# Four modulation quarters: from the end of the front to the head of the stream order

## The chip, the cores and the metric

The kernel runs on one core of a Trainium2 chip, as one launch, with float32 inputs and outputs. The metric is the device time of that launch in microseconds (us). Three runs of the kernel before gave 1077.91, 1078.41 and 1078.48 us; their median is 1078.41 us. One further execution was profiled, and all profile rows of "before" come from it.

The engines are called as in the profile: PE multiplies matrices (PEld loads its weights), DVE works on whole tiles elementwise, ACT applies functions and copies, POOL does a few small operations and issues some transfers, SP issues most transfers. Each engine works through its own list in order; a semaphore wait at the head of a list holds everything behind it.

## The reference, cut to what matters

One layer of a diffusion backbone for 512 latent tokens and 256 context tokens, width 1024:

```python
m_lat = (jax.nn.silu(c) @ mod_w[layer] + mod_b[layer])[:, None, :]     # 1024 x 6144
sh1, sc1, g1, sh2, sc2, g2 = jnp.split(m_lat, 6, axis=-1)
h_lat = rms_norm(x, norm_mix_g) * (1.0 + sc1) + sh1
mix   = token_mixer(h_lat, h_ctx, ...)    # gated DeltaNet (A) and HGRN2 (B), both directions, 4 heads each
x = x + g1 * mix
x = x + g2 * swiglu(rms_norm(x, norm_ffn_g) * (1.0 + sc2) + sh2, ffn_w_in, ffn_w_out)
return rms_norm(x, final_norm_g)
```

The modulation row `m_lat` is the product of one vector with the 1024 x 6144 matrix `mod_w`. Its first two sections (sh1, sc1) are needed at the start, to make `h_lat`. The other four are needed late: g1 (section 2) after the mixer, sh2 and sc2 (3, 4) before the feed-forward part, g2 (5) at the end. These are the **late modulation**. Each section is cut into four **quarters** of 256 columns; a quarter reads 1 MB of weights.

## The kernel before, in words

**Products.** Every large product is done as three passes over a high and a low part of both operands (`mm3`). A weight tile is loaded by SP into `raw`, cast by ACT into `hi` (L103), and DVE makes `lo = raw - hi` (L105); rings of two buffers each.

**The front** (L179 to L407) loads x, ctx and the early part of `mod_w`, makes sh1 and sc1 on PE (`pmod`), makes the normed and modulated tokens transposed (`hhi`, `hlo` for the latent tokens, `chi`, `clo` for the context), and multiplies as it goes six column blocks of the merge gates (`pg0`). At its end, with a priority lowered by 1500, two more gates (22 and 23, tiles `rw`) are multiplied, and then come the four quarters of section 2 (g1). Then the small decay parameters are made (L411 to L468: `pab`, `la`, `dec`).

**A quarter** (`mod_now`) is one transfer of 1 MB, ten DVE operations of 128 x 256 (two products L165, six multiply-adds L167, one sum L168, and the addition to the bias `vc` L176), and in between a short group of PE instructions that sum over partitions (`pmo`, L119) into the PSUM bank "fa". There is one bank "fa"; the low-priority gates (`gate_low`) accumulate in it too. In the front a quarter's transfer is issued by SP, and its tile is one of the six buffers "mw" of the front's pool `s1`. A quarter called by `mod_early` is issued by POOL, and its tile is the single buffer "aT" or "N" of the pool `gd`. These two are otherwise the attention and decay matrices of the DeltaNet pair in work.

**The streams.** After the front, generators are advanced by the string `PLAN`, written out by hand: G0 and G2 are the DeltaNet heads 0, 1 and 2, 3; H0 to H3 the HGRN2 heads; F is a low-priority gate; N and aT are single quarters in those tiles. One number is how many steps are taken. What stands earlier in PLAN has the higher priority. The first six steps of a G stream are the projections k, q, v of two heads with a five-tap convolution and SiLU (DVE L665, L670, L679; ACT L656 to L691); a POOL `memset` clears the borders of each `pad` tile first. Then N and aT are built (L724 to L735), inverted by a recursion on DVE (L754, L756), and six steps over the chunks follow.

**What sets the order.** A list planner simulates the program at build time and fixes the order of each engine's list: among what is ready in its simulation, the highest priority goes first. In its order, a pool that takes the room of an earlier one opens after that one has been finished altogether; the waits left in the program are finer, tile by tile. So the tiles of `fl`, `hg` and `gd` (the streams) are first written, in the planner's order, after the last instruction on the front's pools `s1`, `sp` and `s3`. Within a pool, the buffers lie in the order in which the program first asks for their names. In the kernel before, `gd` begins with KT, QT, Vt, and N and aT come after the convolution buffers ("cv", "blk"). At the end of the streams, `gd` gives its room to `wx` (weights of the remaining gates, loaded by SP), `md` (the remaining quarters, loaded by POOL in halves `mwb`, L906) and `x1p`.

**After the streams:** the gates' remainder, up-projections, output projection, and the feed-forward part, which are bounded by PE.

Of the kernel before, what the change touches and what calls it, by code (L numbers as in the profile page):

```python
# [7 lines left out]
F32 = mybir.dt.float32  # L8
# [5 lines left out]
P = 128  # L14
D = 1024
KT = 8
# [13 lines left out]
PADQ = 8 * 68  # L30
MK = 4

PLAN = ("H0:1 G0:6 F:1 H1:3 G0:4 F:1 G2:3 G0:5 F:2 N:1 G0:1 H0:2 "
        "F:1 G0:99 H0:99 F:3 G2:4 H1:99 G2:4 F:1 G2:99 N:1 H3:99 aT:1 H2:1 X H2:99")


# [15 lines left out]
def body(tc, T, out, tap=None):  # L52
    nc = tc.nc
# [7 lines left out]
    with ExitStack() as root:  # L61
        def pool(name, bufs=1, side=None, **kw):
            return tc.tile_pool(name=name, bufs=bufs, side=side, reuse_waits="tile", **kw)
# [57 lines left out]
        def feat(w, src, n, name, t0=0, tag="mm"):  # L121

            ps = bank(tag, name)
            mm3(ps[:, 0:n], [lambda k, t=t: t[:, k, :] for t in w], [lambda k, t=t: t[:, k, t0:t0 + n] for t in src], KT)
            return ps
# [11 lines left out]
        def gate_out(i, ps, pool, tag="raw"):  # L137
            gt = pool.tile([P, SEQ], F32, name=f"gt{i}", tag=tag, bufs=3 if pool is ring.get("sp") else 2)
            nc.scalar.copy(gt[:, :], ps[:, :])
            nc.sync.dma_start(gdram[i, :, :], gt[:, :])  # L140
# [15 lines left out]
        quarters = [(sec, j) for sec in (2, 3, 4) for j in range(4)]  # L156

        def mod_now(sec, j, mw, queue):

            c0 = D * sec + 256 * j  # L160
            queue.dma_start(mw[:, 0:KT, :], T["mod_w"][0, :, c0:c0 + 256].rearrange("(k p) f -> p k f", p=P))
            for k in range(KT):
                acc = mw[:, k % 2, :]
                if k < 2:
                    nc.vector.tensor_scalar_mul(acc, acc, sc[:, k:k + 1])  # L165
                else:
                    nc.vector.scalar_tensor_tensor(acc, mw[:, k, :], sc[:, k:k + 1], acc, op0=ALU.mult, op1=ALU.add)  # L167
            nc.vector.tensor_tensor(mw[:, 0, :], mw[:, 0, :], mw[:, 1, :], op=ALU.add)  # L168
            mod_sum(sec, j, mw[:, 0, :], "fa")

        def mod_sum(sec, j, acc, tag):
            ps = bank(tag, f"pmo{sec}{j}")
            for i in range(2):
                column_sums(ps, i, acc[:, P * i:P * i + P])
            c = 8 * sec + 2 * j
            nc.vector.tensor_tensor(mbc[:, c:c + 2], ps[:, 0:2], mbc[:, c:c + 2], op=ALU.add)  # L176
# [7 lines left out]
        with ExitStack() as st:  # L184
            s1 = st.enter_context(pool("s1"))
# [216 lines left out]
            for i in rest[0:2]:  # L402
                w = [s1.tile([P, KT, P], F32R, name=f"rw{i}{j}") for j in range(2)]
                w = split([W_IN[:, gcols[i]:gcols[i] + P]], KT, P, dst=[t[:, :, :] for t in w])
                gate_out(i, feat(w, lat, SEQ, f"pgate{i}"), sp, "gt")
            for q in quarters[0:4]:
                mod_now(*q, s1.tile([P, KT, 256], F32, name="mwe%d%d" % q, tag="mw", bufs=6), nc.sync)  # L407
            del quarters[0:4]
            tc.cur_priority -= 1500


# [551 lines left out]

        before, after = PLAN.split("X")
        for item in before.split():
            name, n = item.split(":")
# [26 lines left out]
        for item in after.split():  # L993
            name, n = item.split(":")
# [222 lines left out]
```

## Time and profile before

| | before |
|---|---|
| median of three runs | 1078.41 us (1077.91 to 1078.48) |
| the profiled execution | 1083.86 us |
| its span, first to last instruction | 1082.1 us |
| PE busy / DVE busy / ACT busy | 1013.3 / 648.6 / 551.6 us |
| mean clock granted to PE | 0.978 |

In a row of busy time by stretch, the numbers are the stretch and its length, then for each engine the busy time and, in brackets, the count of instructions; then the clock granted to PE, the share of the transfer engines, and GB/s. In a row of the timeline, they are the start, the length, the engine, the line in the kernel, the operation, what it writes and reads, and, in square brackets, how long the engine had been idle and what ended that. "SPq" is SP issuing a transfer. A row "x6" merges six instructions in a row.

### The profile page before, as it was taken

To read this page: it belongs to the slowest core of one execution; us is meant where nothing else is said; L and a number is where in the kernel's file an instruction comes from. 1 tells how busy PE (TensorE), PEld (TensorE's weight loads), DVE (VectorE), ACT (ScalarE), POOL (GpSimd) and SP (SyncE) were. 2 spreads that over 40 slices of the span, in tenths; PEclk is the share of its full clock that TensorE was granted. 3 is DMA by queue.
4 is the path that set the end of the run, shared out by engine and by line. 5 is a ranking of instruction groups with operands and counts; after the bars stand their busy time and mean duration, and the time that the engine had idled before them with its cause. 6 is when DMAs were issued, how large, how long until landed. Compare 5 with 4: busy or idle time off the path is not lost.

```text
span 1082.1 us, 18148 instructions
## 1 busy us (share of the span) xinstructions
PE 1013.3 (94%) x7255; PEld 830.2 (77%) x7255; DVE 648.6 (60%) x1258; ACT 551.6 (51%) x1053; POOL 72.7 (7%) x129
## 2 busy tenths in 40 slices
PE   4999999889998899899979999999999999999996
PEld 2577888777797687788758788797888878888785
DVE  3375686789666858965786575686343434322524
ACT  3372678558976775786764643442222222221212
POOL 1000000400011012001111000010000000000000
PEclk9999999989999899999998999999999999999998
DMA  9953212113013122201647743445333323333222
GB/s 316 334 182 114 57 48 78 42 48 89 12 51 108 50 69 69 69 3 58 214 129 232 257 153 125 129 151 180 97 98 97 97 80 98 98 98 97 89 97 88
DMA packets 139656, 121.73 MB, mean 112 GB/s; under 512 B 5661, under 2 KB 116531, under 8 KB 139571
## 3 DMA queue, kind: packets, MB, share of 16 engines
q1 hardware_dynamic: 133923, 103.96, 31.4%
q0 software_dynamic: 3552, 13.11, 3.7%
q10 hardware_dynamic: 2096, 3.50, 1.0%
q8 instruction: 57, 0.93, 0.3%
q14 instruction: 28, 0.23, 0.1%
HBM read 110.07 MB, written 10.49 MB: 111 GB/s over the span
## 4 chain that ended last, share of the span: by engine, by line
PE 65%; DVE 12%; ACT 8%; issue 6%; DMA 5%; POOL 2%; SPq 0%; POOLq 0%; DVEq 0%; ACTq 0%
PE pf L113 20%; PE pfo L113 10%; PE h_z L113 5%; PE pgate L113 4%; PE pg L369 3%; PE pup L113 3%; DVE lo L105 2%; PE g_q_zl L113 2%; DMA mwb<-in_mod_w_dram 2%; PE pwo L113 1%; PE g_k_zl L113 1%; DVE p_o L754 1%; PE p_pD L724 1%; ACT hi L103 1%; DVE p_Z L756 1%
## 5 line engine op out<-in xcount | busy, mean ns | idle before, releaser
L103 ACT CAST hi<-raw 128x1024 fp32r<-128x1024 f32 (+1 forms) x129 | 127.6, 991 | 277.3 <-PE pf L113 98.1
L105 DVE TENSOR_TENSOR lo<-raw,hi 128x1024 fp32r<-128x1024 f32 (+1 forms) x129 | 147.8, 1147 | 174.2 <-ACT hi L103 173.9
L113 PE MATMUL pf<-hhi,lo 128*128 128x512 f32 (+1 forms) x352 | 133.8, 380 | 0.5 <-DVE lo L105 0.5
L113 PE MATMUL pf<-hhi,hi 128*128 128x512 f32 (+1 forms) x352 | 133.8, 381 | 0.0
L113 PE MATMUL pf<-hlo,hi 128*128 128x512 f32 (+1 forms) x352 | 133.7, 380 | 0.0
L113 PEld LDWEIGHTS pf<-hhi,lo 128*128 128x128 f32 x352 | 66.2, 188 | 13.7 <-DVE lo L105 1.1
L113 PEld LDWEIGHTS pf<-hlo,hi 128*128 128x128 f32 x352 | 66.2, 188 | 12.5 <-DVE hlo L1097 0.2
L113 PEld LDWEIGHTS pf<-hhi,hi 128*128 128x128 f32 x352 | 66.1, 188 | 12.4
L113 PE MATMUL pfo<-lo,uh 128*128 128x512 f32 x176 | 68.8, 391 | 0.1
L113 PE MATMUL pfo<-hi,ul 128*128 128x512 f32 x176 | 68.5, 389 | 0.0
L113 PE MATMUL pfo<-hi,uh 128*128 128x512 f32 x176 | 67.9, 390 | 0.0
L113 PE MATMUL pgate<-hhi,lo 128*128 128x512 f32 x128 | 54.3, 425 | 6.4 <-DVE lo L105 6.4
L113 PE MATMUL pgate<-hhi,hi 128*128 128x512 f32 x128 | 54.1, 423 | 4.0 <-ACT hi L103 3.9
L113 PE MATMUL pgate<-hlo,hi 128*128 128x512 f32 x128 | 53.0, 414 | 0.0
L1153 DVE TENSOR_TENSOR sg<-sg,pf 128x512 f32<-128x512 f32 x22 | 15.1, 687 | 49.4 <-PE pf L113 49.3
L908 DVE SCALAR_TENSOR_TENSOR acc<-mwb,sc,acc 128x256 f32<-128x256 f32 x72 | 34.2, 480 | 12.6 <-DMA mwb<-in_mod_w_dram 11.5
L113 PE MATMUL h_z<-hhi,hi 128*128 128x512 f32 x96 | 38.6, 402 | 1.3 <-ACT h_Z L515 1.3
L113 PEld LDWEIGHTS pfo<-lo,uh 128*128 128x128 f32 x176 | 33.0, 188 | 7.8 <-DVE lo L105 1.0
L113 PEld LDWEIGHTS pfo<-hi,uh 128*128 128x128 f32 x176 | 32.8, 188 | 7.4 <-ACT hi L103 0.7
L113 PEld LDWEIGHTS pfo<-hi,ul 128*128 128x128 f32 x176 | 33.0, 188 | 6.8
L113 PE MATMUL h_z<-hlo,hi 128*128 128x512 f32 x96 | 37.9, 395 | 0.0
L113 PE MATMUL h_z<-hhi,lo 128*128 128x512 f32 x96 | 37.7, 392 | 0.0
(453 smaller groups left out, 2471.9 us busy)
## 6 DMA issues: line engine op xcount, KB each, us to landing
raw<-in_ffn_w_in_dram SPq DMA_DIRECT2D x44, 512.0 KB, 3.7
raw<-in_w_in_dram SPq DMA_DIRECT2D x37, 512.0 KB, 3.7
raw<-in_ffn_w_out_dram SPq DMA_DIRECT2D x22, 512.0 KB, 3.6
mwb<-in_mod_w_dram POOLq DMA_DIRECT2D x18, 512.0 KB, 4.8
mw<-in_mod_w_dram SPq DMA_DIRECT2D x16, 512.0 KB, 6.0
gdram<-gt SPq DMA_DIRECT2D x24, 256.0 KB, 2.1
raw<-in_w_in_dram SPq DMA_DIRECT2D x18, 256.0 KB, 3.0
mwe<-in_mod_w_dram SPq DMA_DIRECT2D x4, 1024.0 KB, 7.9
```

The costliest lines, as they stand in the source:

```text
L103: nc.scalar.copy(hi[:, :, :], raw[:, :, :])
L105: nc.vector.tensor_tensor(lo[:, :, :], raw[:, :, :], hi.bitcast(F32), op=ALU.subtract)
L113: nc.tensor.matmul(ps, a[u](k), b[v](k), start=(start and n == 0), stop=(stop and n == tot - 1))
L369: nc.tensor.matmul(pg0[i][:, :], u[:, P * i:P * i + P], v[:, d, :], start=(d == 0 and n == 0), stop=(d == KT - 1 and n == 2))
L724: nc.tensor.matmul(pD[:, P * d:P * d + P], (LS, US)[d], lu[:, d, :], start=True, stop=True)
L754: nc.vector.tensor_tensor(ov, Z[:, r + 1:32, r:r + 1].to_broadcast([P, 31 - r, r]), Z[:, r:r + 1, 0:r].to_broadcast([P, 31 - r, r]), op=AL ...
L756: nc.vector.tensor_tensor(Z[:, r + 1:32, 0:r], Z[:, r + 1:32, 0:r], ov, op=ALU.add)
L908: nc.vector.scalar_tensor_tensor(acc[:, :], mw[:, k - k0, :], sc[:, k:k + 1], acc[:, :], op0=ALU.mult, op1=ALU.add)
L1153: nc.vector.tensor_tensor(sg[:, :], sg[:, :], pgu[1][:, :], op=ALU.mult)
```

## The change

The four quarters of section 2 are taken out of the front, and four items are put into PLAN behind H0's first step: one quarter in the tile aT, one in N, and two more in aT. The last four lines of the front that issue them go; the two gates above them stay.

```diff
-PLAN = ("H0:1 G0:6 F:1 H1:3 G0:4 F:1 G2:3 G0:5 F:2 N:1 G0:1 H0:2 "
+PLAN = ("H0:1 aT:1 N:1 aT:2 G0:6 F:1 H1:3 G0:4 F:1 G2:3 G0:5 F:2 N:1 G0:1 H0:2 "
         "F:1 G0:99 H0:99 F:3 G2:4 H1:99 G2:4 F:1 G2:99 N:1 H3:99 aT:1 H2:1 X H2:99")
...
                 gate_out(i, feat(w, lat, SEQ, f"pgate{i}"), sp, "gt")
-            for q in quarters[0:4]:
-                mod_now(*q, s1.tile([P, KT, 256], F32, name="mwe%d%d" % q, tag="mw", bufs=6), nc.sync)
-            del quarters[0:4]
             tc.cur_priority -= 1500
```

The items call a function that was there already:

```python
def mod_early(sec, j, tag):
    mod_now(sec, j, gd.tile([P, 12 if tag == "N" else KT, 256], F32, name=f"mwe{sec}{j}", tag=tag), nc.gpsimd)
```

The list `quarters` is used up in the same order as before, so that the later items N:1, N:1, aT:1 and the remaining quarters are the same ones in both kernels. What moves with a quarter is its transfer (from SP's list to POOL's), its DVE operations, its PE sums, and its tile (from `s1` to `gd`). "aT" and "N" become the first names asked for in `gd`, so every buffer of `gd` up to "blk" gets another place.

## The prediction

> **What bounds the kernel now.** The page first, for the span, the busy shares, the chain that ended last and one kind of transfer.
>
> ```profile
> span 1082.1 us, 18148 instructions
> ...
> PE 1013.3 (94%) x7255; PEld 830.2 (77%) x7255; DVE 648.6 (60%) x1258; ACT 551.6 (51%) x1053; POOL 72.7 (7%) x129
> ...
> PE 65%; DVE 12%; ACT 8%; issue 6%; DMA 5%; POOL 2%; SPq 0%; POOLq 0%; DVEq 0%; ACTq 0%
> ...
> raw<-in_w_in_dram SPq DMA_DIRECT2D x37, 512.0 KB, 3.7
> ```
>
> PE is busy 94% and holds 65% of the chain: time is lost only where PE stands idle or does more. So I went on to busy time by stretch around the change, and one row for what follows.
>
> ```profile
> 70.00:80.00 10.00, 10.00 (x52) 7.72 (x51) 9.92 (x28) 10.00 (x20) 0.00 (x0) 1.00 1.01 327
> ...
> 100.00:110.00 10.00, 9.26 (x75) 8.02 (x75) 3.69 (x7) 5.48 (x10) 0.00 (x0) 0.86 0.30 88
> 110.00:120.00 10.00, 10.00 (x57) 8.77 (x56) 5.63 (x6) 5.99 (x9) 0.00 (x0) 1.00 0.18 52
> 120.00:140.00 20.00, 19.00 (x182) 16.12 (x181) 13.84 (x22) 13.36 (x20) 1.77 (x9) 1.00 0.19 54
> 140.00:160.00 20.00, 20.00 (x149) 16.71 (x148) 16.99 (x26) 16.12 (x25) 1.80 (x4) 1.00 0.19 53
> ```
>
> ```profile
> 200.00:300.00 100.00, 90.66 (x1063) 73.72 (x1063) 82.25 (x177) 73.33 (x149) 12.62 (x24) 0.95 0.17 46
> ```
>
> PE has no idle time from 70 to 80 us, 0.74 us in 100 to 110, 1.0 us in 120 to 140; DVE has much room before 120 and little after (13.84 and 16.99 of 20 us). In 200 to 300 DVE is at 82% and PE loses 9.3 us, in the recursion on DVE: what G0 loses before that is not simply given back there. Next, the same stretches for the quarters' tiles alone, then the timeline where front and streams meet.
>
> ```profile
> 60.00:70.00 10.00, 0.00 (x0) 0.00 (x0) 2.12 (x7) 0.00 (x0) 1.00 0.21 56
> 70.00:80.00 10.00, 0.00 (x0) 0.00 (x0) 4.75 (x13) 0.00 (x0) 1.00 1.01 327
> 80.00:90.00 10.00, 0.00 (x0) 0.00 (x0) 3.62 (x9) 0.00 (x0) 1.00 0.69 222
> 90.00:100.00 10.00, 0.60 (x30) 0.43 (x30) 3.87 (x9) 0.00 (x0) 0.97 0.16 45
> ```
>
> ```profile
> 96.73 0.31 PE L119 MATMUL pmo<-ones,mwe 128*32 128x1 f32 x16
> ...
> 97.18 0.20 DVE L458 TENSOR_TENSOR la<-e,nal 128x48 f32<-128x48 f32 x1
> ...
> 97.45 0.34 SPq L140 DMA_DIRECT2D gdram<-gt  x1
> ...
> 97.55 0.62 PE L465 MATMUL pg<-la,sq 128*128 128x24 f32 x4
> ...
> 103.43 1.05 ACT L103 CAST hi<-raw 128x1024 fp32r<-128x1024 f32 x1 [4.03 <-PE h_z L113]
> ...
> 103.44 0.22 PE L119 MATMUL pmo<-ones,mwe 128*32 128x1 f32 x2
> 103.70 0.16 DVE L176 TENSOR_TENSOR vc<-pmo,vc 128x2 f32<-128x2 f32 x1 [6.32 <-PE pmo L119]
> ...
> 104.38 0.85 ACT L515 COPY h_Z<-h_z 128x512 f32<-128x512 f32 x2
> ...
> 104.50 0.31 PE L119 MATMUL pmo<-ones,mwe 128*32 128x1 f32 x16 [0.29 <-DVE vc L176]
> ...
> 105.01 0.50 PE L113 MATMUL g_k_zl<-hhi,hi 128*128 128x512 f32 x1 [0.20 <-ACT h_Z L515]
> ```
>
> The quarters take 2.12 + 4.75 + 3.62 + 3.87 = 14.36 us of DVE, **3.59 us each**, nearly all while PE has other work. They cost PE two gaps in its own work: 96.73 to 97.55, and 103.44 to 105.01, where their sums stand between the last context product and G0's first projection, each waiting until DVE has emptied the bank of the one before.
>
> **The change part by part.**
>
> **1. Front, PE.** The two stretches go: 0.82 + 1.57 = 2.39 us. The sums themselves stay PE work: four groups of about 0.31 us (the group at 104.50) = 1.24 us, now put between G0's projections, where they wait only if bunched. Net -1.15. For the second stretch there is a condition: 105.01 also waits for ACT's copy of `h_Z` (104.38), which clears the PSUM bank. That copy is the first write into the stream pools, so in the planner's order it comes after everything on the front's pools; the last of that now is the fourth quarter's sum, afterwards it is gate 23's store, issued at 97.45. Then the copy no longer stands behind the cast at 103.43, which had to wait for PE. If it doesn't move, the second stretch is kept and the term is 0.82 - 1.24 = +0.4; if it moves, and H0's and G0's starts with it, as far as the copy can (104.38 back to the store, 97.45: 6.9 us) and half of that reaches the end, -3.5. I take -1.15, because PE is full before and after and can only gain what it did there.
>
> **2. The first two quarters.** Their tiles aT and N become the lowest in `gd`, and by the order of names they lie where the buffers of the early `mod_w` (`mw`) lay.
>
> ```profile
> L313 PE MATMUL pmod<-mw,sch x80: 592/617/1061, 13.7 to 52.8; 128*32 128x512 f32 x48, 128*32 128x256 f32 x32
> ```
>
> PE read those for the last time at 52.8 us, so POOL can issue both loads as soon as its list is past the power at 62.39:
>
> ```profile
> 62.39 0.65 POOL L299 TENSOR_TENSOR ss<-ss,mhalf 128x1 f32<-128x1 f32 x1 [6.32 <-DVE ss L298]
> ...
> 509.04 0.96 POOL L161 DMA_DIRECT2D mwe<-in_mod_w_dram  x1 [0.68 <-PE p_s_pk L864]
> 510.74 1.02 POOL L478 TENSOR_TENSOR p_hs<-p_hs,mhalf 128x4 f32<-128x4 f32 x1 [0.73 <-DVE p_hs L477]
> ...
> 518.02 2.40 POOL L478 TENSOR_TENSOR p_hs<-p_hs,mhalf 128x4 f32<-128x4 f32 x1 [5.36 <-DVE p_hs L477]
> ```
>
> A load from POOL took 509.04 to 515.26 = 6.22 us (next fence). Both are in at about 70. The planner puts their DVE work just behind `la` (97.18), which comes up to 3.87 us sooner, since the stretch 90 to 100 loses that much DVE work. DVE then has 97.38 - 3.87 = 93.5 to 103.70 free (the row at 103.70 shows 6.32 idle): 10.2 us for 7.18. Cost **0**, hidden by the h_z products on PE. If the cover is gone (loads only after the front, landing at 97.45 + 6.2), the 7.18 us fall in 104 to 111 and cost up to that less the DVE idle of 100 to 110 (6.31): +0.9.
>
> **3. The last two quarters.** Both need the one buffer aT, so each waits for the sum of the one before: load (6.22), DVE (3.59), sum, load. From a first sum at about 107, the third's DVE work starts near 114, the fourth's near 125: in the middle of G0's convolutions. There it has priority over all G0 work, being earlier in PLAN, and DVE's list is in order. What a quarter loaded late does to DVE's list the trace shows at the end of the streams:
>
> ```profile
> 515.26 0.62 DVE L165 TENSOR_SCALAR mwe<-mwe,sc 128x256 f32<-128x256 f32 x2 [3.99 <-DMA mwe<-in_mod_w_dram]
> ...
> 520.99 0.62 DVE L165 TENSOR_SCALAR mwe<-mwe,sc 128x256 f32<-128x256 f32 x2 [1.46 <-DMA mwe<-in_mod_w_dram]
> ...
> 528.58 0.15 DVE L176 TENSOR_TENSOR vc<-pmo,vc 128x2 f32<-128x2 f32 x1
> ```
>
> DVE stood 3.99 us for one and 1.46 us for the other before the data was there: the planner expected them sooner. Bounds for the wait 0 and 3.99; I take the mean, 2.7, the two rows being equally near. A late quarter thus holds DVE 3.59 + 2.7 = 6.3 us, both **12.6 us**. Queued behind on DVE are the five-tap convolutions and the `lo` parts, for which ACT and PE wait, as G0's norm sum shows:
>
> ```profile
> 127.25 0.39 PE L113 MATMUL pgate<-hhi,hi 128*128 128x512 f32 x1
> ...
> 134.25 0.43 PE L119 MATMUL g_q_pn<-ones,g_q_acc 128*32 128x1 f32 x32 [0.88 <-ACT g_q_acc L691]
> ```
>
> ```profile
> 100.00:200.00 100.00, 1.83 (x6) 0.98 (x6) 0.00 (x0) 0.99 0.22 62
> ```
>
> Cover: DVE's idle time in 110 to 140 is 4.37 + 6.16 = 10.5 us, but in pieces between operations that depend on each other; I count half, 5.3. Lower bound of the term: all of it used and no landing wait, 7.18 - 10.5 < 0, so 0. Upper: none used and 3.99 each, 15.2. Mine: 12.6 - 5.3 = 7.3. PE has no slack against this chain: at 134.25 it already stands 0.88 us for it. What PE can do meanwhile is the low gate, begun at 127.25. In 100 to 200 it got six products (the last row, gates alone); of its first half, 12 products, six are left, by 13.68 us for 52 (term 4's rows) 0.26 us each, 1.6 us. So **+5.7**.
>
> POOL's list: behind the two late loads stand `memset`s of the `pad` tiles and the powers for G0's norms; each load waits there for the sum before it, and the planner puts it at about that time. No cost of its own; 0 to the length of one delay, inside the bounds above.
>
> On loads from POOL, what the sum does not need. The Trainium skill ("DMA: Bandwidth & Descriptors", Anatomy of one DMA — SWDGE (gpsimd) path) fits 2.0 us + bytes / 436e3 per us, an estimate of 4.4 us for 1 MB; the trace has 6.22, so I keep that, and by the page the term would be about 2 x 1.8 us less. It also states ("SBUF — State Buffer", Who interferes with whom) that a DVE operation in a two-port mode, which `tensor_scalar` can enter, shuts POOL out of its port, descriptors included: the power at 518.02 took 2.40 us during a quarter's DVE work against 1.02 at 510.74, which agrees, and by it the two late loads could be issued 1.4 us later each while DVE is at work.
>
> **4. End of the streams.** The buffers of `wx` now lie over aT and N, and not over KT, QT, Vt. The remaining gates' first load must wait until quarter (3, 2) in aT is summed (528.58, above) and not only for its turn in SP's list:
>
> ```profile
> 523.24 1.88 SPq L95 DMA_DIRECT2D raw<-in_w_in_dram  x2
> ```
>
> That is 5.3 us later. The gates are first multiplied after 540:
>
> ```profile
> 520.00:540.00 20.00, 0.00 (x0) 0.00 (x0) 0.00 (x0) 0.91 0.65 196
> 540.00:560.00 20.00, 13.68 (x52) 9.22 (x52) 1.15 (x2) 1.00 0.50 157
> ```
>
> A load of that kind lands 3.7 us after issue (last row of the first fence), 532.3, with the cast (1.05 at 103.43) and a `lo` of about as much 534.4: **0**, hidden by PE's other work in 520 to 540. Without that cover +5.3. `md`, for its part, no longer lies over N, and may load some us earlier: I know no row for that and leave it at 0, with as much as the load's 5.3 in the other direction as its bound.
>
> **Sum:** -1.15 + 0 + 5.7 + 0 = +4.55 us, against the profiled execution: 1083.86 to 1088.4. The profiled execution is 5.45 us over the median of the runs, 1078.41; the difference carries over: **1083.0 us**.
>
> **The rivals.**
>
> *Hidden after all, 1077.8.* The two late quarters fall into DVE's idle pieces and the planner lets H1's products (next in PLAN) run ahead on PE. For it: 10.5 us of idle against 7.18. Against: the rings of two buffers and the `pad` tiles, which DVE must free, bound how far PE runs ahead. Then only -1.15 and about +0.5 of bunched sums remain.
>
> *Faster, 1074.4.* One mechanism: the front's pools end with gate 23's store and not with the fourth sum, so that H0's copies, G0's first `pad` tiles and G0's first projection start earlier. Place 97 to 105, price -2.39 to -3.5 (term 1), plus up to -0.5 from DVE in 70 to 80, where it is 9.92 of 10 us busy and the context's `lo` parts wait among the quarters. It decides if the late quarters cost the G0 chain under 2 us. For it: PE is full before and after, so PE's gain stays a gain. Against: term 3.
>
> *Twice as slow, 1088.7.* The low gate takes the bank "fa" at 127.25, before the fourth quarter's sum. Then that sum waits for the gate's 18 remaining products (4.7 us), its copy and the sum (1 us), and G0's own aT waits with it:
>
> ```profile
> 187.70 0.41 DVE L735 TENSOR_TENSOR p_aT<-p_E,p_pD 128x256 f32<-128x256 f32 x1
> ```
>
> Before, all four sums were out by 105, ahead of the gate. Here +4.55 + 5.7.
>
> **How the numbers follow.** Forecast 0.45 (1080.6, where no change ends, to 1085.6, with landing waits of 3.99), hidden 0.20, faster 0.20, bank 0.15. What a measurement of this kernel can tell from no change is about 0.2%, 2.2 us. Faster: 0.20 and a little of hidden, 0.23. Same: the rest of hidden and the low end of the forecast, 0.22. Slower: 0.55. Range: from the faster rival's 1074.4 to the bank's 1088.7 and the 2.6 us of longer landing waits, 1074.4 to 1091.
>
> **What would show it.** Right: the first two quarters' DVE work between 93 and 105, loads issued by POOL at about 63; G0's first projection at 102 to 104 instead of 105.01; two runs of quarter work on DVE between 110 and 135 with idle in front ended by their transfer; the sum that stood at 134.25 later by 3 us or more, with more PE idle in 120 to 200. Wrong: those two runs in DVE time that was idle, PE idle in 100 to 200 no larger (hidden, or faster); the loads of the first two only after 97; a sum `pmo` after 180 (bank); or a difference that arises after 500, by term 4.

## The result and the profile after

| | before | after |
|---|---|---|
| median | 1078.45 us (4 runs, 1077.91 to 1079.05) | 1088.05 us (4 runs, 1086.56 to 1090.56) |
| ratio, 95% interval | 1 | 1.0091 (1.0068 to 1.0115) |
| the same again, beside later experiments | 1080.37 us | 1.0102 (1.0081 to 1.0123) |
| the profiled execution, its span | 1083.86, 1082.1 us | 1090.56, 1088.8 us |

The change makes the kernel slower by 9.6 us. The forecast was 1083.0, 4.55 us slower: the sign and the range held, the size was half of it. The profiled executions differ by 6.7 us only; that of before lies 5.4 us over its median, that of after 2.5.

First the busy time of the kernel after by stretch, in the columns of before.

```profile
70.00:80.00 10.00, 7.18 (x32) 5.24 (x31) 3.99 (x10) 6.97 (x14) 0.00 (x0) 0.90 0.98 301
...
100.00:110.00 10.00, 10.00 (x60) 8.87 (x60) 1.98 (x3) 6.21 (x11) 0.16 (x2) 1.00 0.15 47
110.00:120.00 10.00, 10.00 (x86) 8.22 (x84) 9.96 (x23) 5.40 (x8) 1.11 (x5) 1.00 0.34 106
120.00:140.00 20.00, 13.02 (x140) 10.54 (x133) 16.42 (x34) 8.51 (x13) 1.98 (x6) 0.83 0.40 122
140.00:160.00 20.00, 20.00 (x134) 16.76 (x133) 16.46 (x26) 13.42 (x21) 0.87 (x7) 1.00 0.25 67
```

Set against the rows of before, PE has lost 2.82 us in 70 to 80 and 5.98 us in 120 to 140 (13.02 for 19.00), and there the granted clock is 0.83 for 1.00. It has gained 0.74 us in 100 to 110, where the granted clock is 1.00 for 0.86. From 140 to 160 PE is as full as before; from 160 to 200 it loses another 0.8 us. What ended PE's idle time, in us, times, and the longest, for the two places:

```profile
PE pc L264 <- ACT gt L139: 2.8, 1, 2.8
```

```profile
PE pmo L119 <- DVE mwe L168: 4.2, 1, 4.2
PE g_v_zl L113 <- DVE lo L105: 2.2, 1, 2.2
PE g_v_zc L113 <- ACT g_q_pad L653: 0.5, 1, 0.5
```

Now the timeline after, at the first of the two places:

```profile
62.88 2.12 POOL L161 DMA_DIRECT2D mwe<-in_mod_w_dram  x2
...
66.65 1.50 SPq L95 DMA_DIRECT2D raw<-in_w_in_dram  x2
...
70.37 8.13 SPq L140 DMA_DIRECT2D gdram<-gt  x6
...
73.96 1.05 ACT L103 CAST hi<-raw 128x1024 fp32r<-128x1024 f32 x1 [1.26 <-DMA raw<-in_w_in_dram]
...
76.33 1.82 ACT L139 COPY gt<-pg 128x512 f32<-128x512 f32 x3 [1.33 <-DMA gdram<-gt]
```

POOL issues both loads at 62.88, as forecast. But then ACT waits for a gate weight loaded by SP (1.26 us) and for a store that has to leave its buffer (1.33 us), and PE waits for ACT. In the second place:

```profile
110.93 0.96 DVE L519 SCALAR_TENSOR_TENSOR h_sg<-h_Z,h_sg 128x768 f32<-128x768 f32 x1
...
111.81 0.61 DVE L165 TENSOR_SCALAR mwe<-mwe,sc 128x256 f32<-128x256 f32 x2
...
116.08 0.88 POOL L161 DMA_DIRECT2D mwe<-in_mod_w_dram  x1 [13.01 <-PE pmo L119]
...
121.84 0.62 DVE L165 TENSOR_SCALAR mwe<-mwe,sc 128x256 f32<-128x256 f32 x2 [0.33 <-DMA mwe<-in_mod_w_dram]
...
125.71 0.42 DVE L168 TENSOR_TENSOR mwe<-mwe 128x256 f32<-128x256 f32 x1
...
126.18 0.40 PE L119 MATMUL pmo<-ones,mwe 128*32 128x1 f32 x16 [4.23 <-DVE mwe L168]
...
127.55 1.22 DVE L105 TENSOR_TENSOR lo<-raw,hi 128x1024 fp32r<-128x1024 f32 x1
...
128.83 0.79 PE L113 MATMUL g_v_zl<-hhi,lo 128*128 128x512 f32 x1 [2.25 <-DVE lo L105]
...
132.58 0.62 DVE L165 TENSOR_SCALAR mwe<-mwe,sc 128x256 f32<-128x256 f32 x2 [0.47 <-DMA mwe<-in_mod_w_dram]
...
137.45 0.30 PE L119 MATMUL pmo<-ones,mwe 128*32 128x1 f32 x16
...
144.32 0.43 PE L119 MATMUL g_q_pn<-ones,g_q_acc 128*32 128x1 f32 x32
```

The first two quarters' DVE work runs at 111.81, 49 us after its data was asked for and behind H0's `h_sg`, not at 93 to 105. The third quarter arrives almost on time (0.33 us of waiting), but PE comes to its sum in its list 4.23 us before DVE has it. Behind it stands `lo` at 127.55, a weight of G0's next product, for which PE waits another 2.25 us. G0's norm sum, which stood at 134.25, is at 144.32: **10.07 us late**, and most of that stays to the end.

### The profile page after: what moved, and what is told of

Read it like the earlier page. It is cut to its first block, busy times and chain, and to the rows that moved or that the text cites. A ratio compares the mean times of both kernels' runs of the same rounds, so it can differ in the third digit from the quotient of the medians.

```text
span 1088.8 us, 18157 instructions
## 1 busy us (share of the span) xinstructions
PE 1007.9 (93%) x7255; PEld 824.2 (76%) x7255; DVE 650.3 (60%) x1258; ACT 552.3 (51%) x1053; POOL 77.5 (7%) x133
## 4 chain that ended last, share of the span: by engine, by line
PE 60%; DVE 13%; DMA 8%; ACT 8%; issue 7%; POOL 2%; SPq 1%; POOLq 0%; DVEq 0%; ACTq 0%
PE pf L113 18%; PE pfo L113 10%; PE pg L369 3%; PE pup L113 3%; PE h_z L113 3%; PE pgate L113 3%; DMA mwb<-in_mod_w_dram 3%; DVE lo L105 2%; PE g_v_zl L113 2%; PE g_k_zl L113 2%; PE g_q_zl L113 1%; DVE p_o L751 1%; PE p_pD L721 1%; DMA mwe<-in_mod_w_dram 1%; DVE p_Z L753 1%
```

## The experiments

Three points in each trace (one profiled execution of each kernel) tell where time goes: G0's first projection on PE, its norm sum on PE (`g_q_pn`), and the stretch between them, which is the time that the streams' first steps take. The last column is the timed ratio to before, with its interval.

| kernel | first projection | norm sum | stretch | time / before |
|---|---|---|---|---|
| before | 105.0 | 134.3 | 29.2 | 1 |
| after | 105.6 | 144.3 | 38.8 | 1.0091 (1.0068 to 1.0115) |
| after again | 104.8 | 144.3 | 39.5 | 1.0102 (1.0081 to 1.0123) |
| 1 no quarters of section 2 | 100.8 | 130.0 | 29.2 | 0.9993 (0.9976 to 1.0011) |
| 2 two loads alone | 106.4 | 135.6 | 29.2 | 1.0036 (1.0022 to 1.0049) |
| 3 first two quarters, the others left out | 103.4 | 134.7 | 31.3 | 1.0034 (1.0021 to 1.0047) |
| 4 two in the front, two at the head | 101.4 | 133.3 | 31.9 | 0.9990 (0.9974 to 1.0006) |
| 5 as 4, both in one buffer | 101.6 | 138.5 | 36.9 | 1.0016 (1.0000 to 1.0031) |
| 6 loads by SP | 98.7 | 137.5 | 38.8 | 1.0075 (1.0051 to 1.0098) |
| 7 aT, N, aT, N | 104.9 | 144.5 | 39.6 | 1.0161 (1.0134 to 1.0187) |
| 8 sums later | 106.0 | 144.6 | 38.6 | 1.0095 (1.0076 to 1.0113) |
| 9 useless products before the third sum | 106.3 | 147.1 | 40.8 | 1.0142 (1.0121 to 1.0164) |
| 10 lower priority | 101.6 | 130.4 | 28.8 | 1.0169 (1.0149 to 1.0189) |
| 11 layout alone | 103.5 | 132.8 | 29.3 | 1.0004 (0.9990 to 1.0017) |

The theory after the two traces: the early loads cost the front its stall, and the quarters' work in 111 to 136 costs the streams' first steps the rest. The rivals stand with each run.

**1. No quarters.** The common base.

```diff
-PLAN = ("H0:1 aT:1 N:1 aT:2 G0:6 ...
+PLAN = ("H0:1 G0:6 ...
-        quarters = [(sec, j) for sec in (2, 3, 4) for j in range(4)]
+        quarters = [(sec, j) for sec in (3, 4) for j in range(4)]
```

> The four quarters of section 2 are left out altogether (g1 is then only its bias; the rest of the computation is as in the kernel after). This is the common base: the kernel before less this is what the quarters cost in the front, the kernel after less this what they cost at the head. Theory (the head's cost is DVE and PE time taken from G0's first steps, 120 to 145 us): base 1074 to 1077, so 2 to 4 us in the front and 11 to 14 at the head; PE busy in 120 to 140 at 18.5 or more of 20 us, as before (19.00; after: 13.02). Rival (the planner's new order of the rest, not the quarters' own work, costs the time): base 1083 or more, PE short in 120 to 140 too.

The stretch is 29.2 us, that of before, so the rest of the program is not slow by its new order; that rival falls. G0's first projection comes 4.2 us earlier than before. In the timed runs that is little: 0.9993, at most 2.6 us less than before by its interval. So **in the front the four quarters cost little or nothing**, at most the low end of the 2 to 4 us expected, and leaving them out altogether wins no more than that.

**2 and 3. The first two, and their loads alone.** Run 3 leaves the other two out; run 2 leaves out the work of all four, but keeps the first two transfers and one DVE operation of two columns on each.

```diff
 # run 3
-PLAN = ("H0:1 aT:1 N:1 aT:2 G0:6 ...
+PLAN = ("H0:1 aT:1 N:1 G0:6 ...
-... for sec in (2, 3, 4) for j in range(4)]
+... for sec in (2, 3, 4) for j in range(4) if (sec, j) not in ((2, 2), (2, 3))]
 # run 2, besides
+            if sec == 2:
+                nc.vector.tensor_scalar_mul(mw[:, 0, 0:2], mw[:, 0, 0:2], sc[:, 0:1])
+                return
```

> The first two quarters go to the head as in the kernel after (both loads from POOL at about 63 us, one in aT, one in N); the other two of section 2 are left out (half of g1 is then only its bias). Theory (the first two cost in the front, where their loads meet SP's; the late ones cost between 105 and 145): PE busy in 70 to 80 is short of 10 again by 2 to 3 us, G0's first projection at 104 to 106 (105.56 after, 100.80 without any quarter), and from there to G0's norm sum only some 2 us more than without quarters; time 1.003 to 1.006 of the kernel before. Rival (only the late ones cost): G0's first projection at 101 to 102, time as the kernel before, 0.998 to 1.001.

> Without any quarter of section 2 (g1 is only its bias), but with the first two loads of the head: POOL issues them at about 62 us into aT and N, and one DVE operation of 2 columns reads each. No sums, no products. It differs from the run without quarters by the two transfers alone. Theory (the transfers, among SP's loads and stores of 60 to 80 us, cost the front its 2.8 us of PE idle): PE busy in 70 to 80 at 7 to 7.5, G0's first projection at 103 to 105 (100.80 without quarters, 103.4 with two head quarters done in full), time 1.002 to 1.004 of before. Rival (it is the two quarters' DVE work and sums that cost the 0.4% of that run): PE busy 70 to 80 at 9.8 or more, projection at 101, time as without quarters, 0.998 to 1.001.

Both have the stall of the front, and both take the same time. The two transfers by themselves cost 0.0036 + 0.0007 = 0.43% over run 1, **4.6 us** (some 2 to 7 by the two intervals); the two quarters' DVE work and sums add nothing that can be measured in the time, though the stretch is 2.1 us longer. In the two traces it does not show at the norm sum either (134.7 for 135.6), because run 3 reached the first projection 3.0 us earlier: PE stood for 2.9 us in both fronts, but the clock granted after it fell in run 2 (0.86 in 70 to 80, then the first row) and not in run 3 (1.00 in 70 to 80, then the second):

```profile
80.00:90.00 10.00, 10.00 (x48) 7.62 (x47) 4.25 (x11) 4.94 (x10) 0.22 (x4) 0.80 0.44 124
```

```profile
80.00:90.00 10.00, 10.00 (x55) 6.71 (x55) 4.07 (x10) 4.16 (x9) 0.22 (x4) 1.00 0.40 115
```

What the early loads cost at that point is thus 2.6 us without a fall of the clock (run 3 against run 1) and 5.6 with one (run 2). How the transfers do it is seen in the rows by kind of transfer (KB each, median us to landing; 55 to 75 us) and in SP's timeline, first for run 1, then for run 2:

```profile
raw<-in_w_in_dram SPq DMA_DIRECT2D x3, 512.0 KB, 4.1
```

```profile
66.06 1.50 SPq L95 DMA_DIRECT2D raw<-in_w_in_dram  x2
...
69.79 5.08 SPq L140 DMA_DIRECT2D gdram<-gt  x6
```

```profile
mwe<-in_mod_w_dram POOLq DMA_DIRECT2D x2, 1024.0 KB, 7.2
raw<-in_w_in_dram SPq DMA_DIRECT2D x2, 512.0 KB, 7.3
```

```profile
66.00 1.50 SPq L95 DMA_DIRECT2D raw<-in_w_in_dram  x2
...
69.73 8.15 SPq L140 DMA_DIRECT2D gdram<-gt  x6
```

SP's 512 KB weights land after 7.3 us instead of 4.1, and its six stores keep SP 8.15 us instead of 5.08: that is ACT's wait for `raw` and for the store's buffer in the timeline of the kernel after. Before, the transfer engines were as full in 70 to 80 (1.01), but a quarter's load stood behind the gate's weights and the first stores in SP's own list, not beside them:

```profile
66.85 1.50 SPq L95 DMA_DIRECT2D raw<-in_w_in_dram  x2
...
70.57 1.33 SPq L140 DMA_DIRECT2D gdram<-gt  x3
...
71.96 0.55 SPq L161 DMA_DIRECT2D mwe<-in_mod_w_dram  x1
```

This is what the prediction never asked: whom the early loads hold up. The Trainium skill ("DMA: Bandwidth & Descriptors", Queues, rings and completion order) states that each transfer engine takes turns between the queues it has work for; a weight that takes nearly twice its time beside another queue's load agrees.

**4 and 5. Two at the head, without and with the chain.** The first two quarters stay in the front. The edits are against the kernel before.

```diff
-PLAN = ("H0:1 G0:6 ...
+PLAN = ("H0:1 aT:1 N:1 G0:6 ...      # run 4
+PLAN = ("H0:1 aT:2 G0:6 ...          # run 5
-            for q in quarters[0:4]:
+            for q in quarters[0:2]:
...
-            del quarters[0:4]
+            del quarters[0:2]
```

> The first two quarters stay in the front as in the kernel before, the last two go to the head, one in aT and one in N; so no load has to wait for another quarter's sum. Theory (the third and fourth quarter, each late behind the sum of the one before, carry most of it): 1078.5 to 1082, sums out by 121, no PE idle of 4 us in front of a sum, G0's norm sum that stands at 134.25 before and 144.32 after at 134 to 138. Rival 1 (each quarter at the head costs alike): half of the difference, 1083 to 1084. Rival 2 (what costs is the first two loads, issued by POOL at 63 us among SP's): nearly all of it, 1085 or more, with the 2.8 us of PE idle at 75 to 78 us there again.

> As the run with two quarters in the front and two at the head, but both of the head use the one buffer aT, so that the second's load waits for the sum of the first. It differs from that run by the chain alone: POOL issues the first load at about 99 again. Theory (a quarter that comes late, in the middle of G0's convolutions, costs more than one that comes early): the second's DVE work at 120 to 124, with a landing wait or PE idle of 2 to 4 us at its sum; G0's norm sum at 137 to 139 (134.0 there), time 3 to 5 us longer, 1.002 to 1.004 of before. Rival (the number of quarters at the head counts, not their lateness): norm sum at 134 to 135, no difference in time.

With part of the quarters in the front, aT and N are not filled early: POOL waits for the front's last `vc` and issues at 98.84; the transfer is in just when DVE comes to it:

```profile
98.84 1.94 POOL L161 DMA_DIRECT2D mwe<-in_mod_w_dram  x2 [36.65 <-DVE vc L176]
...
107.35 0.35 DVE L165 TENSOR_SCALAR mwe<-mwe,sc 128x256 f32<-128x256 f32 x1 [0.57 <-DMA mwe<-in_mod_w_dram]
```

Run 4 costs nothing that can be measured: 0.9990. So half of the change is free when its loads are kept out of the front's traffic and none waits for a sum. Both rivals of that run fall. The chain alone, which moves the second quarter's DVE work from 111 to 115 us to 122 to 126, lengthens the stretch by 5.0 us and the time by 0.26%, 2.8 us (the intervals of the two runs overlap a little). The waits are at the sums, as expected:

```profile
112.89 0.31 PE L119 MATMUL pmo<-ones,mwe 128*32 128x1 f32 x16 [1.38 <-DVE mwe L168]
...
126.05 0.31 PE L119 MATMUL pmo<-ones,mwe 128*32 128x1 f32 x16 [2.28 <-DVE mwe L168]
```

**6. Loads by SP.** The order on DVE and PE stays nearly that of the kernel after.

```diff
-                    mod_early(*quarters.pop(0), name)
+                    mod_early(*quarters.pop(0), name, nc.sync if len(quarters) >= 8 else nc.gpsimd)
```

> As the kernel after, but SP issues the head quarters' loads, so that the first two go out behind gate 23's store, at about 100 us, and not at 63. Theory (the two early loads from POOL fall among SP's loads and stores of 60 to 80 us and cost PE 2.8 us there): PE busy in 70 to 80 is 9.8 or more again (7.18 after), DMA share of 60 to 70 is 0.25 or less (0.52 after), la at 97.5 or earlier (98.92 after); but the first two quarters then land at about 106 and DVE waits for them with h_K and the convolutions behind: 1085 to 1087. Rival (the front's stall is made good before 105, so it is worth nothing): 1088 to 1090.

The front's stall is gone (PE 10.00 in 70 to 80), and the first projection, at 98.7, is 6.9 us earlier than after. The transfer engines' share in 60 to 70 stays at 0.51, now by SP's own weights, which it issues from 63.91 on instead of 66.65; so part of the 6.9 us is another order of the front, and the projection is even 2.1 us ahead of run 1. The stretch is 38.8, as long as after: up to the norm sum, the loss at the head does not depend on the loss in the front. In the time little of the front's gain is left: 1.0075 lies 1.7 to 2.9 us below the two timings of the kernel after, and the intervals overlap. So this run shows what ends the stall, but not that the stall is worth 4.6 us of time here.

**7. Four quarters, two buffers in turn.**

```diff
-PLAN = ("H0:1 aT:1 N:1 aT:2 G0:6 ...
+PLAN = ("H0:1 aT:1 N:1 aT:1 N:1 G0:6 ...
```

> As the kernel after, but the four quarters take aT, N, aT, N in turn, so the third and fourth load wait for the first and second sum and are in flight together. Theory (the chain is the cost): fourth sum at 127 to 130 instead of 137.45, G0's norm sum at 139 to 141 instead of 144.32, time 3 to 5 us below the kernel after: 1.004 to 1.006 of before. Rival 1 (15 us of DVE work ahead of the convolutions is the cost, chained or not): norm sum at 143 to 145, 1.008 to 1.010. Rival 2 (four back to back block DVE longer in one piece): norm sum later than 146, over 1.010.

The theory of the chain falls: the third and fourth load are in flight together, the fourth sum comes at 129.97 instead of 137.45, and the stretch is no shorter. The timeline:

```profile
125.56 0.39 PE L119 MATMUL pmo<-ones,mwe 128*32 128x1 f32 x16 [4.25 <-DVE mwe L168]
...
129.97 0.39 PE L119 MATMUL pmo<-ones,mwe 128*32 128x1 f32 x16 [4.02 <-issue]
...
130.69 0.80 PE L113 MATMUL pgate<-hhi,hi 128*128 128x512 f32 x1 [0.33 <-DVE vc L176]
```

The two sums now stand close together, and PE stands 4.25 and 4.02 us for them, with the low gate's products behind. (For the second the view names no releaser; DVE's last operation for that sum is at 129.46, of 0.42 us.) So the wait of the fourth load for the third sum is not what costs. The third and fourth loads still wait for the sums of the first and second (POOL issues them at 115.39 and 119.75), and their DVE work, at 121 to 130, still lies among G0's convolutions. That late place costs, as in run 5, and not the chain by itself. The time is longer than that of the kernel after by 0.59 to 0.70%, rival 2's range, though the norm sum is not later (144.5 for 144.3); by the first write of the streams' own aT, 202.0 for 198.1, 3.9 us of it are there. What loses them no run separates.

**8. Sums later.** Each quarter's result goes to spare rows of N, and the sums come after G0's six steps (item S).

```diff
-PLAN = ("H0:1 aT:1 N:1 aT:2 G0:6 F:1 ...
+PLAN = ("H0:1 aT:1 N:1 aT:2 G0:6 S:1 F:1 ...
...
+            if sec == 2:
+                qa = keep[:, 8 + j, :]
+                nc.vector.tensor_tensor(qa, mw[:, 0, :], mw[:, 1, :], op=ALU.add)
+                sums.append((sec, j, qa))
+                return
             nc.vector.tensor_tensor(mw[:, 0, :], mw[:, 0, :], mw[:, 1, :], op=ALU.add)
             mod_sum(sec, j, mw[:, 0, :], "fa")
...
+            if name == "S":
+                for sec, j, qa in sums:
+                    mod_sum(sec, j, qa, "fa")
```

> As the kernel after, but each quarter's last DVE operation puts its result into rows of the N tile that no load uses, and the four sums on PE come after G0's first six steps in the order. So PE no longer stands in its list at a sum that DVE has not finished, and aT comes free when DVE is done with it. Theory (PE's stand of 4.23 us in front of the third sum is half of what is lost at 120 to 140): PE busy in 120 to 140 at 16 to 18 (13.02 after), time 1.004 to 1.006 of before. Rival (PE only stands there because the weights' lo and the convolutions are queued behind the quarters on DVE; without the sum it stands at the next product): PE busy 13 to 15, 1.007 to 1.010.

The rival holds by the time, 1.0095: without those sums in its list, PE waits longer, at the next product that needs DVE's results (and is busy for only 11.7 of the 20 us in 120 to 140, under the rival's 13 to 15). That product waits for ACT, and ACT for DVE:

```profile
PE g_k_pn L119 <- ACT g_k_acc L694: 7.4, 1, 7.4
```

```profile
136.54 0.84 ACT L694 ACTIVATE g_k_acc<-g_KT 128x768 f32<-128x768 f32 x1 [4.36 <-DVE g_KT L685]
```

So **DVE is what PE stands for**; the sum at 126.18 is only the first place in PE's list where it shows.

**9. Useless products in the idle time.**

```diff
             ps = bank(tag, f"pmo{sec}{j}")
+            for _ in range(16 if (sec, j) == (2, 2) else 0):
+                nc.tensor.matmul(ps[:, 4:508], hhi[:, 0, 0:P], hlo[:, 0, 0:504], start=True, stop=True)
```

> As the kernel after, with 16 more products of 128 x 504 on PE ahead of the third quarter's sum, into columns of its bank that nothing reads: about 3.5 us of useless work in the place of 4.23 us of PE idle. Theory (the idle costs twice: the 4.23 us and then products at a lower granted clock, 0.83 in 120 to 140, the first ones at 0.79 us instead of 0.39): the idle in front of that sum falls under 1.5 us, the granted clock of 120 to 140 rises to 0.92 or more, G0's norm sum comes 1 to 2.5 us earlier than 144.32, the time falls by 1 to 2.5 us: 1.006 to 1.008 of before. Rival (the clock falls for another reason, or the lost time is on DVE anyway): norm sum at 144 to 146, time 1.008 to 1.011.

A miss for theory and rival alike: the norm sum, 147.1, and the time, 1.0142, lie above both ranges. The idle time in front of the sum fell to 1.27 us as expected, but the granted clock of 120 to 140 did not rise (0.83, as after), its fall came later: 0.91 in 120 to 130, then

```profile
130.00:140.00 10.00, 10.00 (x61) 8.14 (x62) 7.27 (x16) 2.74 (x4) 0.22 (x4) 0.75 0.62 191
```

Around the sum PE still had 1.27 and 2.34 us of idle within 3.9 us (125.57 to 129.48). The clock's share in the loss is thus not shown by taking it away; it is read off the durations below.

**10. Lower priority.**

```diff
+                    low = 3000 if len(quarters) > 8 else 0
+                    tc.cur_priority += low
                     mod_early(*quarters.pop(0), name)
+                    tc.cur_priority -= low
```

> As the kernel after, but the four head quarters have a priority lower by 3000, so that the planner puts G0's convolutions and H0 ahead of them on DVE and PE. Theory (their rank on DVE is the cost): two thirds of the difference go, 1081 to 1084; what is left is the front's stall (2.8 us of PE idle at 75 to 78). Rival 1 (the waits for loads and sums cost it, whatever the rank): 1086 to 1089. Rival 2 (late quarters hold back G0's own aT at 187 us): 1088 or more, with sums pmo after 150.

The stretch is 28.8, as short as without quarters: in the stretch, the quarters' rank was indeed the cost. The front's stall is gone too, since POOL now issues the first two loads at 99.65, which the expectation did not foresee. But then the third sum, of low rank on a full PE, is done only at 197.8 us, though DVE had its part ready at 137; the fourth load waits for that sum, and G0's own aT, first written at 198.1 in the kernel after, for that:

```profile
198.40 0.95 POOL L161 DMA_DIRECT2D mwe<-in_mod_w_dram  x1 [12.11 <-PE pmo L119]
...
204.47 0.61 DVE L165 TENSOR_SCALAR mwe<-mwe,sc 128x256 f32<-128x256 f32 x2 [5.06 <-DMA mwe<-in_mod_w_dram]
...
210.24 0.75 DVE L732 TENSOR_TENSOR p_aT<-p_E,p_pD 128x256 f32<-128x256 f32 x2 [0.61 <-PE pmo L119]
```

That is rival 2 of the expectation, and the dearest of all: 1.0169.

**11. Layout alone.** In the kernel before, aT and N are asked for first.

```diff
+        for tag, m in (("aT", KT), ("N", 12)):
+            z = gd.tile([P, m, 256], F32, name="z" + tag, tag=tag)
+            nc.gpsimd.memset(z[:, 0, 0:1], 0.0)
```

> The kernel before, with aT and N asked for first in the pool gd (a POOL memset of one column each), so that every buffer of gd lies as in the kernel after while the quarters stay in the front. It is the layout alone. Theory (the layout by itself moves only the end of the streams, where nothing was seen to change): 0.998 to 1.002 of before. Rival (the layout delays the remaining gates' loads at the end of the streams, by up to 5.3 us): 1.003 to 1.005, the difference arising after 500.

No difference in time. The remaining gates' first load does come later, as term 4 had it, and is hidden:

```profile
526.45 1.01 SPq L95 DMA_DIRECT2D raw<-in_w_in_dram  x2
```

It stood at 523.24 before, where the profile of this run is otherwise 2 to 3 us ahead of before.

**The kernel after again**, as a measure beside runs 2, 9 and 11:

> The kernel after once more, beside the others, as their common measure: 1.007 to 1.011 of before, PE idle of 4 us in front of the third sum, granted clock 0.80 to 0.88 in 120 to 140.

The time, 1.0102, and PE's idle, 4.1 us, came as expected; the clock in 120 to 140 did not, it was 0.74, lower still than the first time.

## Why the prediction was right and wrong

Of the signs that the prediction named for itself, the loads at about 63, the two late runs of quarter work with idle in front ended by their transfer, and the norm sum late by more than 3 us came. Two failed: the first two quarters' work at 93 to 105 (it ran at 111.81) and the projection at 102 to 104 (105.56).

The delay of the norm sum, 144.32 - 134.25 = 10.07 us, is set against the prediction's terms. Its parts are 105.56 - 105.01 = 0.55 in the front and 38.76 - 29.24 = 9.52 in the stretch.

**Term 1, the front, -1.15 forecast, +0.55 measured.** The gain was there, and larger: without quarters the first projection is 4.2 us earlier, beyond the bound of 3.5. Some 1.5 us of that is likely the clock, for which the term has nothing: the profile of before has 0.86 in 100 to 110, and run 11, with the quarters in the front and 1.00 there, reaches the projection at 103.5, 2.7 us after run 1, which is near the 2.39 of the term. The early loads took the gain back (4.6 us by time; at that projection 2.6 us in run 3 and 5.6 in run 2, over run 1). The step that failed is in term 2: "Both are in at about 70", priced as if a load in time nobody computes in costs nothing. The row that spoke against it stood in the prediction: 70.00 to 80.00 with a DMA share of 1.01.

**Term 2, the first two quarters, 0 forecast, 2.1 us of stretch measured** (run 3), and nothing measurable in time (run 3 less run 2). Its place was wrong: the work did not follow `la` but `h_sg` at 110.93. I had the loads' issue by the waits that are left in the program, and DVE's order as if the planner knew of that early issue. That the planner, which opens `gd` only after the front, expected the data later is the likely reason, though no run shows it.

**Term 3, the last two, +5.7 forecast, 38.8 - 31.3 = 7.5 measured** (after less run 3; in time 0.57 to 0.68%, 6.2 to 7.3 us). The mechanism was right: DVE work of first rank in the middle of G0's convolutions. Two sizes in it were off, each in its own direction. The landing wait was 0.33 and 0.47 us where I took 2.7: the rows at the end of the streams were not like this place. The 1.4 us by which the late loads could go out later, taken from the power at 518.02, did not show: POOL took 0.88 us for each (116.08 and 126.91), and at 518.02 DVE was in multiply-adds and `h_K`, its two `tensor_scalar` of that quarter being at 515.26. And the filler of 1.6 us did not come: the low gate shares the bank "fa" with the sums and ran first in 154, behind the fourth of them, so that it did nothing here where it had done six products before:

```profile
120.00:140.00 20.00, 0.00 (x0) 0.00 (x0) 0.00 (x0) 0.83 0.40 122
140.00:160.00 20.00, 0.86 (x3) 0.56 (x3) 0.00 (x0) 1.00 0.25 67
```

Two things I had no term for. PE stood at the sum and at `lo`, 4.23 + 2.25 us in a row, and after that stand its products were slower. The products of G0's v projection alone, before and after (25 products before, 24 after, in 100 to 145):

```profile
100.00:145.00 45.00, 5.70 (x25) 4.78 (x26) 0.57 (x1) 0.97 0.23 67
```

```profile
100.00:145.00 45.00, 7.65 (x24) 5.73 (x24) 0.57 (x1) 0.92 0.29 88
```

7.65 - 5.70 = 1.95 us more for one product less. The 9.52 us are so accounted for, by estimate: PE idle 6.98 instead of 0.88 after the first projection, +6.1; slower products, +2; the four sums, which I had counted in term 1, +1.24; the rest is order (some more of the next head's products run ahead, the gate's six do not).

**Term 4, 0 forecast, 0 measured** (run 11).

**The rivals.** *Hidden* fell: where the quarters stood DVE had hardly any idle time left (9.96 us busy in 110 to 120). *Faster* had its mechanism, the front's end, but the loads used it up. *Bank* had the right bank and the wrong victim: the gate waited for the sums. The time that it would have given, 1088.7, is near the result by another cause. In run 10 G0's aT does wait for a late quarter, but by its rank.

**From the norm sum to the end.** The first and the last write of the streams' own aT (in the rows, the times after the comma), before and after:

```profile
L735 DVE TENSOR_TENSOR p_aT<-p_E,p_pD x16: 406/421/423, 187.7 to 410.8; 128x256 f32<-128x256 f32 x16
```

```profile
L732 DVE TENSOR_TENSOR p_aT<-p_E,p_pD x16: 409/421/422, 198.1 to 419.2; 128x256 f32<-128x256 f32 x16
```

The first is 10.4 us late, the last, of the second pair, 8.4, the end of the profiled executions 6.7. "Not simply given back" was right for most of it. Where the 3.7 us between the first write and the end were given back is not shown: PE idles less in 320 to 360 (1.60 for 4.84 us), but more in 360 to 400 (4.83 for 1.39), as the same work lies later.

## What to carry to other kernels

A transfer moved into time where its data's buffer is free is not free itself: look at the share of the transfer engines there, and at whose loads and stores it will stand beside, before giving it the price nought. Work moved to the head of a hand-written order takes its rank with it: on a full engine with work on both sides of it, ask what stands behind it in that engine's list, and remember that lowering its rank can hurt a later user of its buffer more. When PE waits in its list for another engine, moving the instruction that it waits at only moves the wait; take the other engine's work away instead, as run 4 does.

## What the runs showed of the hardware

**PE's clock after a stand.** After 4.23 and 2.25 us of idle with little between, the first product took 0.79 us (the row at 128.83) and the next ones 0.63; 128 x 512 products take 0.39 otherwise:

```profile
129.42 0.63 PE L113 MATMUL g_v_zl<-hhi,hi 128*128 128x512 f32 x1
```

In run 7, with 4.25 and 4.02 us nearly in a row, the granted clock was 0.56 in 130 to 140; in run 9, 1.27 and 2.34 us within 3.9 us sufficed for 0.75. In run 5 stands of 1.38 and 2.28 us, 13 us apart, left it at 1.00:

```profile
100.00:145.00 45.00, 40.20 (x321) 34.25 (x321) 32.64 (x54) 27.33 (x38) 3.85 (x21) 1.00 0.40 117
```

A single stand in the front did both: after 2.8 us in the kernel after the clock was 0.93 in 80 to 90, after 2.9 us it was 0.80 in run 2 and 1.00 in run 3. The kernel before shows 0.86 in 100 to 110 with no more than 0.28 us of idle in the ten us before, behind two sums and twelve narrow products of 24 columns. So no length of a stand comes out of these runs below which the clock stays. Where it fell, it cost about 2 us besides the stand in the kernel after (the products of v) and some 3 us in run 2 (against run 3, at the first projection). The Trainium skill ("TensorE: Matmul & The Clock Gate", What's actually happening) states that the clock is halved after at least one idle window of some 3.4 us and comes back after at least as long a time of work. The doubled duration agrees, and so, roughly, does the time of work: from the first work after the stand to the full clock, some 3 us in the front of the kernel after and 6.5 us in run 2. The length of the stand does not: here 2.8 us sufficed in one trace, and 2.9 us did not in another.

**Two queues side by side.** Two loads of 1 MB from POOL made SP's 512 KB loads land after 7.3 us (median of two) instead of 4.1 (median of three) in runs 1 and 2, which differ by these loads and two DVE operations of two columns.
